# A decoder layer in seven-product block matmuls: the scheme carried from the down projection to gate and up

## The chip, the core and the metric

One core of a Trainium2 chip runs the whole kernel. The metric is device time in microseconds (us) of one execution. TensorE is called PE here, its weight loads PEld, VectorE is DVE, ScalarE is ACT, GpSimd is POOL, and SP issues most DMAs.

## The reference

256 tokens of width 2048 pass one layer: a normalised input projection, a convolution group and an attention group, an output projection, and a SwiGLU feed-forward part of width 5632. Only the last part is touched by the change.

```
x = x + rmsnorm(mix, post_mix_norm)
hf = rmsnorm(x, pre_ffn_norm)                                  # 256 x 2048
ff = (silu(hf @ w_gate) * (hf @ w_up)) @ w_down                # 5632 wide inside
x = x + rmsnorm(ff, post_ffn_norm)
```

## The kernel before

**Precision.** Every weight and every activation is split into two float16 parts, a high part (ACT, a scaled copy) and a low part (DVE, scaled source minus high part). One product of a 128x128 activation block with a 128x512 weight block is then three matmuls: high x high, high x low, low x high (`mm3`, and `mm` in the down part). Weight tiles of 1 MB are loaded by SP into `st` (pool `stage`, 4 buffers) and split into `whi` and `wlo` (pool `wsp`, 8 buffers each, 2048 columns). A `whi`/`wlo` buffer comes free when PE has done the last matmul that reads it, an `st` buffer when DVE has read it last.

**Gate and up.** The loop over `j` takes 22 groups of 512 columns, 256 of gate beside 256 of up. Each group needs 16 blocks of the inner dimension (`k`), for two token blocks (`tb`), so 96 matmuls per group, into two of the four PSUM tiles of `ps_acc`. The first two groups run ahead on token block 0 (`LEAD`), while token block 1 of `hf` is still being normalised, split and transposed by DMA. `swiglu(j, ps)` reads the two PSUM tiles, multiplies, splits, and has the result transposed by DMA into `aT`. For ten groups (`FAST`: 0, 2, ... 18) it also forms the sums of activation blocks that the down part needs.

**Down.** Two passes `u` over 1024 output columns each take 22 pairs of inner blocks. A pair of inner blocks, two token blocks and two halves of the columns make a 2x2 by 2x2 block product: eight block products done plainly (`plain`), so 24 matmuls. For the ten pairs in `FAST` Winograd's scheme does it in seven (21 matmuls): some products go into the result tiles `E`, four others (`X, Y, Z, Q`) into the tiles of `ps_tmp`, and four additions on DVE at the end (`fix`) distribute them. It needs sums of weight blocks: `load_pair` splits three blocks as they come (1536 columns), adds blocks in place in `st` (three DVE additions, L730 to L732), and splits the four results (2048 columns). Pairs alternate, a fast one and then a plain one; the last three are plain.

**Order.** A scheduler orders each engine's instructions at build time; each engine then works through its own list in order, and waits on semaphores for the others. A DVE instruction that waits holds all DVE work behind it.

Of the kernel before, what the change touches and what calls it, by code (L numbers as in the profile page):

```python
# [47 lines left out]
A_S = 8.0  # L48


@with_exitstack
def hymba_layer(ctx: ExitStack, tc: tile.TileContext, x, xT, pos, inv_freq, g_pre, w_in, w_lat,
# [15 lines left out]
    arena = const.tile([P, 70 * KB], F32, name="arena")  # L68
# [185 lines left out]
    rs = rstd_of(ss_t, D, 2)  # L254
    nc.vector.tensor_scalar(r_x, rs, 1.0 / (W_S * X_S), None, op0=ALU.mult)
# [324 lines left out]

    mxc_of = flat(mx_h[:, :CB], mx_l[:, :CB])
    x_off = dram.tile([P, NTB, D], F32, name="x_off")
    r_f = const.tile([P, NTB], F32, name="r_f")
    for tb in range(NTB):
# [13 lines left out]
        for j in range(4):  # L598
# [4 lines left out]
            gx = work.tile([P, 512], F32, tag="ss", name=nm("gxf"), bufs=3)  # L603
# [20 lines left out]
    hw3 = region(50, (2, 3, P), F16)  # L624

# [3 lines left out]
    def fast_of(j):  # L629
# [5 lines left out]
    def swiglu(j, ps):  # L635
        fast = j in FAST
        for tb in range(NTB):
            r = r_f[:, tb : tb + 1]
            sg = work.tile([P, 256], F32, tag="A", name=nm("sg"), bufs=3)
            nc.scalar.activation(sg, ps[tb][:, 0:256], AF.Silu, scale=r)  # L640
# [4 lines left out]
            nc.vector.scalar_tensor_tensor(a, ps[tb][:, 256:512], r, sg, op0=ALU.mult, op1=ALU.mult)  # L645
# [15 lines left out]
    LEAD = 2  # L661
    lead = []
    for j in range(NG):
        wgt = Weights(KD, 512).load(w_gu[j], W_S)
        ps = [acc_tile(), acc_tile()]
        if j < LEAD:
            mm3(ps[0:1], hf_of, wgt, (0,))
            lead.append((wgt, ps))
            if j == LEAD - 1:
                for i, (wgt, ps) in enumerate(lead):  # L670
                    mm3(ps[1:2], hf_of, wgt, (1,))
                    swiglu(i, ps)
        else:
            mm3(ps, hf_of, wgt)
            swiglu(j, ps)
# [6 lines left out]
    ssd = const.tile([P, NTB, 4], F32, name="ssd")  # L682

    def down_out(tb, j, ps, f):
        cs = slice(j * 512, (j + 1) * 512)
        nc.vector.tensor_tensor(f, ps, f, op=ALU.add)
# [4 lines left out]

    r_fin = {}
# [192 lines left out]
```

## Time and profile before

| what | value |
|---|---|
| median of three runs | 1016.5 us (1015.99 to 1017.17) |
| the profiled execution | 1016.03 us, of which its span 1014.2 us |
| PE busy | 975.7 us, 4652 matmuls |
| DVE, ACT busy | 742.5 us, 532.5 us |

The span runs from the first to the last instruction in the trace. Stages by the trace: input projection, convolution and attention up to about 250 us, output projection to about 327 us, gate and up to 784 us, down to about 1001 us, and the last normalisation.

### The profile page before, as it was taken

How to read it: one execution, taken by the hardware profiler on the slowest of the kernel's cores; microseconds unless marked ns; L12 is line 12 of the kernel's file. 1: busy time of each engine (PE TensorE's matmuls, PEld its weight loads, DVE VectorE, ACT ScalarE, POOL GpSimd, SP SyncE). 2: the span in 40 equal slices, each digit the busy share in tenths (PEclk: the TensorE clock that was granted, in tenths of full speed). 3: DMA queues.
4: the chain of work that ended last, by engine and by line, in shares of the span. 5: the costliest groups of instructions: out<-in, count | busy, mean ns of one | idle time of the engine just before them, and what ended most of it. 6: DMA issues, size and time to landing. Idle time of an engine off the chain costs nothing.

```text
span 1014.2 us, 11941 instructions
## 1 busy us (share of the span) xinstructions
PE 975.7 (96%) x4652; PEld 462.3 (46%) x4652; DVE 742.5 (73%) x860; ACT 532.5 (53%) x599; POOL 37.7 (4%) x50
## 2 busy tenths in 40 slices
PE   6999997999999999999999999999999999989996
PEld 2444553774444444444444444444444444434442
DVE  6699999999868886555455555555556788888787
ACT  7796665664746564454444444454443544554551
POOL 0000000034100100000000000000000000000000
PEclk9999998999999999999999999999999999999998
DMA  9874666576546998676766776777755555635453
GB/s 348 330 256 140 223 209 196 166 241 222 201 166 170 321 303 290 218 228 201 240 217 206 222 224 223 226 218 217 234 198 166 176 189 224 235 127 222 166 186 145
DMA packets 77769, 220.37 MB, mean 217 GB/s; under 512 B 49552, under 2 KB 50192, under 8 KB 55184
## 3 DMA queue, kind: packets, MB, share of 16 engines
q1 hardware_dynamic: 76992, 218.68, 64.2%
q10 hardware_dynamic: 720, 0.93, 0.3%
q8 instruction: 36, 0.59, 0.2%
q14 instruction: 21, 0.17, 0.1%
HBM read 204.25 MB, written 4.19 MB: 206 GB/s over the span
## 4 chain that ended last, share of the span: by engine, by line
PE 64%; DVE 18%; issue 5%; ACT 5%; POOL 2%; DMA 1%; DVEq 0%; POOLq 0%; ACTq 0%; SPq 0%
PE acc L146 16%; PE acc L145 16%; PE acc L144 16%; DVE wlo L100 7%; DVE arena L277 3%; PE acc L749 3%; PE acc L750 3%; PE acc L748 3%; ACT whi L99 3%; DVE st L730 1%; PE tmp L749 1%; PE tmp L750 1%; PE tmp L748 1%; POOL sm L198 1%; DVE arena L285 1%
## 5 line engine op out<-in xcount | busy, mean ns | idle before, releaser
L100 DVE SCALAR_TENSOR_TENSOR wlo<-st,whi 128x2048 f16<-128x2048 f32 (+4 forms) x211 | 451.7, 2157 | 203.3 <-ACT whi L99 203.3
L99 ACT ACTIVATE whi<-st 128x2048 f16<-128x2048 f32 (+4 forms) x211 | 376.2, 1800 | 320.7 <-PE acc L146 176.5
L144 PE MATMUL acc<-whi,arena 128*128 128x512 f16 (+1 forms) x1084 | 410.1, 378 | 5.5 <-ACT whi L99 5.5
L145 PE MATMUL acc<-wlo,arena 128*128 128x512 f16 (+1 forms) x1084 | 410.4, 379 | 3.9 <-DVE wlo L100 3.8
L146 PE MATMUL acc<-whi,arena 128*128 128x512 f16 (+1 forms) x1084 | 409.8, 378 | 0.0
L144 PEld LDWEIGHTS <-arena 128*128 128x128 f16 x1084 | 106.7, 98 | 130.2 <-ACT arena L104 4.9
L146 PEld LDWEIGHTS <-arena 128*128 128x128 f16 x1084 | 106.7, 98 | 129.6 <-issue 6.9
L145 PEld LDWEIGHTS <-arena 128*128 128x128 f16 x1084 | 106.5, 98 | 125.2 <-issue 2.5
L748 PE MATMUL acc<-whi,arena 128*128 128x512 f16 x232 | 87.9, 379 | 0.0
L749 PE MATMUL acc<-wlo,arena 128*128 128x512 f16 x232 | 87.9, 379 | 0.0
L750 PE MATMUL acc<-whi,arena 128*128 128x512 f16 x232 | 87.9, 379 | 0.0
L277 DVE SCALAR_TENSOR_TENSOR arena<-arena 128x256 f32<-128x256 f32 x184 | 78.0, 480 | 0.0
L640 ACT ACTIVATE sg<-acc,r_f 128x256 f32<-128x256 f32 x44 | 20.7, 473 | 58.8 <-PE acc L146 58.8
L749 PEld LDWEIGHTS <-arena 128*128 128x128 f16 x272 | 26.6, 98 | 32.3 <-issue 0.3
L748 PEld LDWEIGHTS <-arena 128*128 128x128 f16 x272 | 26.6, 98 | 32.1
L750 PEld LDWEIGHTS <-arena 128*128 128x128 f16 x272 | 26.6, 98 | 32.1
L283 ACT ACTIVATE x_sb<-arena 128x256 f32<-128x256 f32 x56 | 25.2, 506 | 11.7 <-DVE arena L285 11.7
L705 POOL TENSOR_TENSOR sm<-sm,neg_half 128x1 f32<-128x1 f32 x2 | 1.1, 541 | 657.0 <-DVE sm L703 657.0
L730 DVE TENSOR_TENSOR st<-st 128x1024 f32<-128x1024 f32 x20 | 24.5, 1224 | 0.6
L153 PE MATMUL tmp<-arena,whi 128*128 128x256 f16 x80 | 21.8, 273 | 0.0
L154 PE MATMUL tmp<-arena,whi 128*128 128x256 f16 x80 | 21.8, 273 | 0.0
L155 PE MATMUL tmp<-arena,wlo 128*128 128x256 f16 x80 | 21.8, 273 | 0.0
(186 smaller groups left out, 610.1 us busy)
## 6 DMA issues: line engine op xcount, KB each, us to landing
st<-in_w_gu SPq DMA_DIRECT2D x88, 1024.0 KB, 5.0
st<-in_w_dn SPq DMA_DIRECT2D x44, 1024.0 KB, 4.9
st<-in_w_out SPq DMA_DIRECT2D x16, 1024.0 KB, 5.1
st<-in_w_in SPq DMA_DIRECT2D x14, 1024.0 KB, 9.3
st<-in_w_lat SPq DMA_DIRECT2D x12, 896.0 KB, 5.0
x_sb<-in_x SPq DMA_DIRECT2D x4, 1024.0 KB, 8.7
st<-in_w_uqn SPq DMA_DIRECT2D x4, 768.0 KB, 4.9
st<-in_w_uv SPq DMA_DIRECT2D x2, 1024.0 KB, 6.0
```

Source lines behind the costliest of these rows:

```text
L99: nc.scalar.activation(hi, src, AF.Copy, scale=scale)
L100: nc.vector.scalar_tensor_tensor(lo, src, scale, hi, op0=ALU.mult, op1=ALU.subtract)
L144: nc.tensor.matmul(p_ap, xh, wh, start=(start and k == 0), stop=False)
L145: nc.tensor.matmul(p_ap, xh, wl, start=False, stop=False)
L146: nc.tensor.matmul(p_ap, xl, wh, start=False, stop=(stop and k == wgt.kt - 1))
L153: nc.tensor.matmul(ps, wh[:, c0 : c0 + P], xh, start=(k == 0), stop=False)
L277: nc.vector.scalar_tensor_tensor(cacc[:, cb, :], upad[:, cb, k : k + S], cw[:, cb, k : k + 1], cacc[:, cb, :], op0=ALU.mult, op1=ALU.add)
L283: nc.scalar.activation(t[:, i, :], upad[:, cb, k : k + S], AF.Copy, scale=cw[:, cb, k : k + 1])
L730: nc.vector.tensor_tensor(st[:, 0:4:3, :], st[:, 0:2, :], st[:, 3:4, :].to_broadcast([P, 2, 512]), op=ALU.add)
L748: nc.tensor.matmul(ps, ah, bh, start=key not in begun, stop=False)
L749: nc.tensor.matmul(ps, ah, bl, start=False, stop=False)
L750: nc.tensor.matmul(ps, al, bh, start=False, stop=last)
```

## The change

Gate and up are regrouped from 22 groups of 512 columns into 11 units of 1024 columns (`NU`; a unit is two groups `j`). A unit takes 8 pairs of inner blocks, and its weights come as 1 MB per pair, four blocks of 512 columns. In five units (`GU_UNITS`: 1, 3, 5, 7, 9) five of the eight pairs (0 to 4) go through the seven-product scheme; the other pairs and units stay plain. Three things come with it. The sums of `hf` blocks are formed and transposed once, in `hf_sums`, called between token block 0 and token block 1 of unit 0. The `Feed` class makes the weight parts in a set order (blocks of this pair and of the next one before the sums of this pair), and chains these instructions on ACT and on DVE so that the scheduler can't reorder them among themselves. `Unit` takes its result tiles in turn from `ps_acc` and `ps_tmp`, and its four extra tiles from the other pool. In a fast unit the pairs come in the order 5, 0, 1, 6, 2, 3, 4, 7, so a plain one first. In the down part a plain pair now comes ahead of each fast one, and two plain pairs in place of three are kept for the end.

```diff
+NU = NG // 2
+GU_UNITS = (1, 3, 5, 7, 9)
+GU_FAST = 5
...
+    row_s = const.tile([P, NTB], F32, name="row_s")
+    nc.vector.tensor_scalar(row_s, rs, 1.0, None, op0=ALU.min)
...
+    def sized(tb, j):
+        cs = slice(j * 512, (j + 1) * 512)
+        gx = work.tile([P, 512], F32, tag="ss", name=nm("gxf"), bufs=3)
+        nc.vector.scalar_tensor_tensor(gx, x_sb[:, tb, cs], row_s[:, tb : tb + 1], g_pf[:, cs], op0=ALU.mult, op1=ALU.mult)
+        return gx
...
-            nc.vector.tensor_tensor(gx, xs, g_pf[:, cs], op=ALU.mult)
-            split(hl[:, 0, :], hl[:, 1, :], gx, X_S)
+            split(hl[:, 0, :], hl[:, 1, :], sized(tb, j), X_S)
...
+    def hf_sums(c):
+        g0, g1 = [sized(tb, c).rearrange("p (i k t) -> p i k t", i=2, k=2) for tb in range(NTB)]
+        sm = region(44, (4, 2, P))
+        for d, p, m in ((0, g1[:, :, 0], g1[:, :, 1]), (1, g0[:, :, 0], g1[:, :, 0]),
+                        (2, g0[:, :, 0], sm[:, 0]), (3, g0[:, :, 1], sm[:, 2])):
+            nc.vector.tensor_tensor(sm[:, d], p, m, op=ALU.subtract)
+        hl = region(48, (2, 8 * P), F16)
+        split(hl[:, 0, :], hl[:, 1, :], sm.rearrange("p s i t -> p (s i t)"), X_S)
+        nc.sync.dma_start_transpose(hS[:, c], hl.rearrange("p a n -> p (a n)"))
...
+        def blocks(self, k):
+            src, scale, fast = self.pairs[k]
+            st = stage.tile([P, 2048], F32, tag="stage", name=nm("st")).rearrange("p (b n) -> p b n", b=4)
+            nc.sync.dma_start(st, src)
+            self.parts[k] = self.split(st, 1536 if fast else 2048, scale)
+            if fast:
+                b12 = st[:, 3:4, :].to_broadcast([P, 2, 512])
+                for d, p, m in ((st[:, 0:4:3, :], st[:, 0:2, :], b12), (st[:, 1, :], st[:, 0, :], st[:, 1, :]),
+                                (st[:, 2, :], st[:, 1, :], st[:, 2, :])):
+                    self.chain("DVE", nc.vector.tensor_tensor(d, p, m, op=ALU.add))
+                self.st[k] = st
+        def get(self, k, ahead=1):
+            for n in range(k, min(k + ahead + 1, len(self.pairs))):
+                if n not in self.parts:
+                    self.blocks(n)
+            parts = self.parts[k]
+            if k in self.st:
+                parts = parts + self.split(self.st.pop(k), 2048, self.pairs[k][1])
+            return parts
...
+            mine, other = (acc_tile, tmp_tile) if Unit.count % 2 == 0 else (tmp_tile, acc_tile)
...
+        def fast(self, blocks, w, last):
+            if self.sums is None:
+                self.sums = [self.other() for _ in range(4)]
+            X, Y, Z, Q = self.sums
+            A22, A11, A12, S1, S3, S2, S4 = blocks
+            self.mm(self.E[0][0], (0, 0), A12, w[2])
+            self.mm(self.E[0][1], (0, 1), S4, w[1])
+            self.mm(X, "X", A11, w[0], last)
+            self.mm(Y, "Y", S2, w[4], last)
+            self.mm(Z, "Z", S3, w[6], last)
+            self.mm(Q, "Q", S1, w[3], last)
+            self.mm(self.E[1][0], (1, 0), A22, w[5])
...
-    LEAD = 2
-        wgt = Weights(KD, 512).load(w_gu[j], W_S)
-            mm3(ps, hf_of, wgt)
-            swiglu(j, ps)
+    gu_order = [GU_FAST, 0, 1, GU_FAST + 1] + list(range(2, GU_FAST)) + list(range(GU_FAST + 2, KP))
+        if u == 0:
+            ws = [feed.get(i, 0) for i in range(KP)]
+            for tb in range(NTB):
+                for i, w in enumerate(ws):
+                    for c in range(2):
+                        unit.plain(i, w, tb, c, i == KP - 1)
+                if tb == 0:
+                    for c in range((GU_FAST + 1) // 2):
+                        hf_sums(c)
...
-    order = [i for f, s in zip(FAST, slow) for i in (f, s)] + slow[len(FAST) :]
+    order = [i for f, p in zip(FAST, slow) for i in (p, f)] + slow[len(FAST) :]
-    TAIL = 3
+    TAIL = 2
```

How the instructions stand on two engines, at the two places of which the prediction speaks. A row names a line, an operation, the output and inputs (with the tile's number) and the size; in brackets it names what the instruction waits for. The line numbers are those of each kernel.

DVE before, where the first two groups of gate and up end: splits of group 2 (L100), then the gates of the first two groups' results (L645) and the first sum of activation blocks (L655).

```order
L100 SCALAR_TENSOR_TENSOR wlo_3224<-st_3221,whi_3223 128x2048 [waits DMAHW1_49,Activation_49]
L100 SCALAR_TENSOR_TENSOR wlo_3230<-st_3227,whi_3229 128x2048 [waits DMAHW2_49,Activation_49]
L100 SCALAR_TENSOR_TENSOR wlo_3236<-st_3233,whi_3235 128x2048 [waits DMAHW3_49,Activation_49]
L645 SCALAR_TENSOR_TENSOR arena<-acc_2970,r_f,sg_3144 128x256 [waits Activation_49]
L645 SCALAR_TENSOR_TENSOR a_3207<-acc_3043,r_f,sg_3205 128x256 [waits Activation_49]
L655 TENSOR_TENSOR arena<-arena 128x128 [waits DVE_49]
```

DVE after, in the same stretch, at the end of unit 0: unit 1's first splits (L695), the additions in `st` (L709), the sums of `hf` (L669, L109), and the gates of unit 0 (L796). `wlo_3312` holds the weight sums of unit 1's first fast pair.

```order
L695 SCALAR_TENSOR_TENSOR wlo_3305<-st_3302,whi_3304 128x1536 [waits DMAHW3_49,Activation_49]
L709 TENSOR_TENSOR st_3302<-st_3302 128x2x512 [waits DVE_49]
L109 SCALAR_TENSOR_TENSOR arena<-arena 128x1024 [waits DMAHW4_49,Activation_49]
L709 TENSOR_TENSOR st_3302<-st_3302 128x512 [waits DVE_49]
L796 SCALAR_TENSOR_TENSOR arena<-acc_2950,r_f,sg_3227 128x256 [waits DVE_49]
L709 TENSOR_TENSOR st_3302<-st_3302 128x512 [waits DVE_49]
L695 SCALAR_TENSOR_TENSOR wlo_3312<-st_3269,whi_3311 128x2048 [waits PE_49]
L695 SCALAR_TENSOR_TENSOR wlo_3343<-st_3340,whi_3342 128x2048 [waits DMAHW1_49,Activation_49]
L796 SCALAR_TENSOR_TENSOR arena<-acc_2952,r_f,sg_3230 128x256 [waits Activation_49]
L796 SCALAR_TENSOR_TENSOR a_3245<-acc_2951,r_f,sg_3243 128x256 [waits Activation_49]
```

The first fast pair's splits, the sums of `hf` and the gates of unit 0 now stand in one line on DVE, and the gate of `acc_2951` (token block 0, second half) is the last row here; before, the gates of the first groups stood behind plain splits alone.

DVE before, one round of the down loop: a plain pair (`wlo_7017`), the blocks of a fast pair (`wlo_7047`), its three additions, its sums (`wlo_7054`).

```order
L100 SCALAR_TENSOR_TENSOR wlo_7017<-st_7014,whi_7016 128x2048 [waits DMAHW2_49,Activation_49]
L100 SCALAR_TENSOR_TENSOR wlo_7047<-st_7044,whi_7046 128x1536 [waits DMAHW3_49,Activation_49]
L730 TENSOR_TENSOR st_7044<-st_7044 128x2x512 [waits DVE_49]
L731 TENSOR_TENSOR st_7044<-st_7044 128x512 [waits DVE_49]
L732 TENSOR_TENSOR st_7044<-st_7044 128x512 [waits DVE_49]
L100 SCALAR_TENSOR_TENSOR wlo_7054<-st_7044,whi_7053 128x2048 [waits Activation_49]
```

DVE after, one round of the same loop: the blocks of a fast pair (`wlo_7340`), its additions, the next plain pair (`wlo_7373`), then the sums (`wlo_7377`).

```order
L695 SCALAR_TENSOR_TENSOR wlo_7340<-st_7337,whi_7339 128x1536 [waits DMAHW1_49,Activation_49]
L709 TENSOR_TENSOR st_7337<-st_7337 128x2x512 [waits DVE_49]
L709 TENSOR_TENSOR st_7337<-st_7337 128x512 [waits DVE_49] x2
L695 SCALAR_TENSOR_TENSOR wlo_7373<-st_7370,whi_7372 128x2048 [waits DMAHW2_49,Activation_49]
L695 SCALAR_TENSOR_TENSOR wlo_7377<-st_7337,whi_7376 128x2048 [waits Activation_49]
```

The plain pair's split moved from ahead of the blocks to between the additions and the sums. PE's own list is 150 rows shorter, 75 matmuls and their 75 weight loads.

## Rows read from the trace of the kernel before

**Rows 1.** The page's span and busy line (busy us, share, count).

```profile
span 1014.2 us, 11941 instructions
...
PE 975.7 (96%) x4652; PEld 462.3 (46%) x4652; DVE 742.5 (73%) x860; ACT 532.5 (53%) x599; POOL 37.7 (4%) x50
```

**Rows 2.** Windows: busy us and count of PE, PEld, DVE, ACT, POOL; clock, DMA share, GB/s.

```profile
400.00:500.00 100.00, 100.00 (x465) 45.36 (x464) 54.58 (x48) 44.78 (x40) 0.00 (x0) 1.00 0.70 219
790.00:840.00 50.00, 50.00 (x233) 22.67 (x232) 41.28 (x30) 21.22 (x13) 0.00 (x0) 1.00 0.59 212
890.00:940.00 50.00, 46.77 (x217) 21.02 (x216) 40.66 (x34) 25.08 (x22) 0.00 (x0) 1.00 0.44 169
```

**Rows 3.** Waits of PE from 280 to 1000 us (total, times, longest).

```profile
PE acc L748 <- DVE m L686: 3.2, 1, 3.2
PE acc L145 <- DVE wlo L100: 1.5, 1, 1.5
PE tmp L749 <- DVE wlo L100: 1.1, 1, 1.1
```

**Rows 4.** Groups of instructions by line and shape (count; busy us, mean ns; idle before).

```profile
L100 DVE SCALAR_TENSOR_TENSOR wlo<-st,whi 128x2048 f16<-128x2048 f32 x165 | 375.8, 2290 | 197.3 <-ACT whi L99 197.3
...
L100 DVE SCALAR_TENSOR_TENSOR wlo<-st,whi 128x1536 f16<-128x1536 f32 x24 | 42.0, 1752 | 4.7 <-ACT whi L99 4.7
...
L730 DVE TENSOR_TENSOR st<-st 128x1024 f32<-128x1024 f32 x20 | 24.5, 1224 | 0.6
...
L732 DVE TENSOR_TENSOR st<-st 128x512 f32<-128x512 f32 x20 | 13.8, 692 | 0.7
...
L645 DVE SCALAR_TENSOR_TENSOR a<-acc,r_f,sg 128x256 f32<-128x256 f32 x24 | 11.5, 482 | 10.2 <-ACT sg L640 10.2
...
L100 DVE SCALAR_TENSOR_TENSOR wlo<-st,whi 128x1024 f16<-128x1024 f32 x8 | 9.7, 1218 | 0.9 <-ACT whi L99 0.9
...
L601 DVE SCALAR_TENSOR_TENSOR x_sb<-arena,sm,x_sb 128x512 f32<-128x512 f32 x8 | 5.7, 747 | 1.1 <-POOL sm L198 1.1
...
L389 DVE TENSOR_TENSOR qt<-zq,sincos 128x256 f32<-128x256 f32 x2 | 0.8, 416 | 0.0
```

**Rows 5.** DVE's timeline where gate and up begin (start us, us).

```profile
327.95 2.28 DVE L100 SCALAR_TENSOR_TENSOR wlo<-st,whi 128x2048 f16<-128x2048 f32 x1
330.15 0.74 DVE L591 SCALAR_TENSOR_TENSOR arena<-acc,r_c,arena 128x512 f32<-128x512 f32 x1
...
344.32 2.28 DVE L100 SCALAR_TENSOR_TENSOR wlo<-st,whi 128x2048 f16<-128x2048 f32 x1
...
349.81 0.15 DVE L612 TENSOR_SCALAR r_f<-sm 128x1 f32<-128x1 f32 x1 [0.66 <-POOL sm L198]
```

**Rows 6.** PE's timeline there.

```profile
346.65 0.38 PE L145 MATMUL acc<-wlo,arena 128*128 128x512 f16 x1 [1.47 <-DVE wlo L100]
```

**Rows 7.** DMA issues: KB each, median us to landing.

```profile
st<-in_w_gu SPq DMA_DIRECT2D x88, 1024.0 KB, 5.0
...
arena<-arena SPq DMA_TRANSPOSE x14, 5.7
```

**Rows 8.** The chain that ended last, one round of the down loop (start us, us).

```profile
942.19 3.96 DVE wlo L100 x2
...
948.97 1.92 ACT whi L99
...
953.12 3.96 DVE wlo L100 x2
```

**Rows 9.** Windows (columns as in rows 2) around two waits of PE.

```profile
160.00:164.00 4.00, 1.00 (x3) 0.51 (x4) 2.87 (x15) 3.66 (x9) 1.16 (x2) 0.55 0.53 189
164.00:168.00 4.00, 4.00 (x13) 1.61 (x12) 4.00 (x11) 1.04 (x2) 0.00 (x0) 0.59 0.34 65
894.00:896.00 2.00, 0.34 (x2) 0.19 (x2) 2.00 (x3) 1.39 (x2) 0.00 (x0) 1.00 0.04 8
```

More of the change, by code (lines that the diff above doesn't have):

```diff
@@ L67, in hymba_layer @@
     KB = 256
[L68 removed]
+    arena = const.tile([P, 82 * KB], F32, name="arena")
     def region(kb, shape, dtype=F32):
@@ new lines, in hymba_layer, with __init__, chain, split @@
+    class Feed:
+        def __init__(self, pairs):
+            self.pairs = pairs
+            self.parts = {}
+            self.st = {}
+            self.last = {}
+        def chain(self, engine, ins):
+            if engine in self.last:
+                tc.add_manual_dep(ins.ins, self.last[engine].ins.name, NO_SYNC, reason="feed order")
+            self.last[engine] = ins
+        def split(self, st, n, scale):
+            hi = wsp.tile([P, 2048], F16, tag="whi", name=nm("whi"))
+            lo = wsp.tile([P, 2048], F16, tag="wlo", name=nm("wlo"))
+            src = st.rearrange("p b n -> p (b n)")[:, :n]
+            self.chain("ACT", nc.scalar.activation(hi[:, :n], src, AF.Copy, scale=scale))
+            self.chain("DVE", nc.vector.scalar_tensor_tensor(lo[:, :n], src, scale, hi[:, :n],
+                                                             op0=ALU.mult, op1=ALU.subtract))
+            return [(hi[:, c : c + 512], lo[:, c : c + 512]) for c in range(0, n, 512)]
+        def blocks(self, k):
[17 more added lines that the diff above has]
+            return parts
@@ L636, in swiglu @@
+    def swiglu(j, unit, c):
         fast = j in FAST
@@ L715, in final @@
             (nc.sync if j % 2 == 0 else nc.scalar).dma_start(out[tb * P : (tb + 1) * P, cs], xs)
-    def parts_of(st, n):
-        hi = wsp.tile([P, 2048], F16, tag="whi", name=nm("whi"))
-        lo = wsp.tile([P, 2048], F16, tag="wlo", name=nm("wlo"))
-        split(hi[:, :n], lo[:, :n], st.rearrange("p b n -> p (b n)")[:, :n], WD_S)
-        return [(hi[:, c : c + 512], lo[:, c : c + 512]) for c in range(0, n, 512)]
-    def load_pair(u, i):
-        st = stage.tile([P, 2048], F32, tag="stage", name=nm("st")).rearrange("p (b n) -> p b n", b=4)
-        nc.sync.dma_start(st, w_dn[u, i])
-        if i not in FAST:
-            return parts_of(st, 2048)
-        parts = parts_of(st, 1536)
-        nc.vector.tensor_tensor(st[:, 0:4:3, :], st[:, 0:2, :], st[:, 3:4, :].to_broadcast([P, 2, 512]), op=ALU.add)
-        nc.vector.tensor_tensor(st[:, 1, :], st[:, 0, :], st[:, 1, :], op=ALU.add)
-        nc.vector.tensor_tensor(st[:, 2, :], st[:, 1, :], st[:, 2, :], op=ALU.add)
-        return parts + parts_of(st, 2048)
@@ L788, in hymba_layer @@
+        unit = Unit(a_of)
+        k0 = NU * KP + u * NG
+        for n, i in enumerate(order[:-TAIL]):
+            w = feed.get(k0 + n)
+            if i in FAST:
+                unit.fast(a_fast(i), w, i == FAST[-1])
+            else:
+                unit.plain_all(i, w)
+        tail = [(i, feed.get(k0 + NG - TAIL + n)) for n, i in enumerate(order[-TAIL:])]
         if u == 1:
@@ L791, in hymba_layer @@
                 nc.sync.dma_start(x_back[tb], x_off[:, tb, :])
-        i, w = tail[0]
         for tb in range(NTB):
             for c in range(2):
-                plain(i, w, tb, c)
-        for tb in range(NTB):
-            for c in range(2):
-                for i, w in tail[1:]:
-                    plain(i, w, tb, c, i == order[-1])
-                down_out(tb, 2 * u + c, E[tb][c], fix[tb][c])
+                for i, w in tail:
+                    unit.plain(i, w, tb, c, i == order[-1])
+                down_out(tb, 2 * u + c, unit.block(tb, c))
                 if u == 1 and c == 0:
```

138 lines of the change are left out of this document (74 added, 64 removed).

## The prediction

> **What bounds the kernel now.** First the page's busy line: PE is busy 96% of the span, DVE 73%, ACT 53% [rows 1]. A share is a mean over stages, so next the windows. From 400 to 500 us, in gate and up, PE is busy without a gap and starts 465 matmuls in 100 us, one per 0.215 us, at granted clock 1.00, its upper level of 2.4 GHz; in the first half of the down part it is the same 233 in 50 us [rows 2]. In these stretches DVE is busy 55% and 83%, DMA 70% and 59%. So PE sets the time here, and a matmul less is 0.215 us less, as long as nothing else comes late. PE's waits between 280 and 1000 us are the list of what is late today: 1.5 us for a weight split where gate and up begin, 3.2 us at the border of the two down passes, 1.1 us near the end of the second [rows 3].
>
> **The change part by part.**
>
> *Matmuls.* 5 units x 5 pairs x one block product x 3 matmuls = 75 fewer. 75 x 0.215 = 16.1 us less, all on the engine that bounds.
>
> *Where DVE has to follow.* A plain pair costs DVE one split of 2048 columns, 2.29 us; a fast one a split of 1536 (1.75), additions of 1.22 and twice 0.69, and a split of 2048 (2.29), 6.65 us in all [rows 4]. Back to back, instructions start about 0.08 us closer than their durations (327.95 to 330.15 is 2.20 for one of 2.28 [rows 5]). A fast unit thus asks 5 x 6.4 + 3 x 2.2 = 39 us of DVE for weights, plus some 11 us for gates, sums and the eight additions of the scheme, 50 us against PE's 177 x 0.215 = 38.1. A plain unit asks 8 x 2.2 + 5 = 23 us against 192 x 0.215 = 41.3. Two units together: 73 of 79.4 us. DVE can do it if it works ahead during the plain unit. I followed one such border in the two engines' lists. With eight `whi`/`wlo` buffers, DVE has everything ready up to the blocks of pair 2 when PE begins a fast unit (call that 0). The gates of the unit before, with their subtractions and splits, hold DVE to about 3.6; then blocks of 3 (4.3, to 8), sums of 2 (2.2, to 10), blocks of 4 (14.5), sums of 3 (17), pair 7 (19). The sums of 4 need the buffer that pair 6 gives back at 19, and then ACT's 1.9 and DVE's 2.2: 24. PE wants the three sums at 21, 26 and 30. So units 3, 5, 7 and 9 lose nothing by it. The border behind a fast unit holds too: the four extra tiles are read about 5 us after the last product into them, and PE spends that time on pair 7.
>
> *Unit 1, where nothing could be done ahead.* Unit 0 holds all eight buffers until its second pass, and DVE has the sums of `hf` to make in that very stretch. DVE's list from the last split of unit 0 to the gate of token block 0, second half, whose PSUM tile product Y of the first fast pair wants: nine operations of 512 columns on `hf` (0.67 or 0.61, 5.9 us), twelve subtractions of 256 (at most 0.35 by the 0.42 of L389: 4.2), three splits of 1024 (1.15: 3.4), three of 2048 (6.6), two of 1536 (3.3), additions 2 x 1.24 and 4 x 0.7 (5.3), three gates (0.40: 1.2), small ones with a wait for POOL (0.9): 30.8 us [rows 4, 5]. In the trace that last split starts at 344.3 and PE goes on at 346.65 [rows 5, 6]; I take 347.0, since seven multiplications ahead of it turn into the three-operand form (0.75 in place of 0.69). So 377.8 without any stall. PE, from 347.0: 11 matmuls of the first pass, 96 of the second, 24 of pair 5 and 9 of the first fast pair, 140 x 0.215, wants the tile at 377.1. From there DVE needs 22.5 us more to the sums of pair 3 (the rest of unit 0's gates and splits 3.0, the blocks of pairs 2, 3 and 4 with their additions 3 x 4.3, the sums of pairs 1, 2 and 3 3 x 2.2): 400.3. PE's second pass ends at 370.0, and 24 + 21 + 21 + 24 + 21 + 9 = 120 matmuls later, at 395.8, it wants them. The loss in unit 1 is then some 4.5 us without any stall. More comes from ACT: the second and third split of `hf` sums reuse one buffer, which must have been transposed by DMA first. No row shows a transpose of 2048 columns; the ones of half the width and less land 5.7 us after issue [rows 7]. At that figure ACT waits some 1 to 2 us for each, and DVE behind it in part; at twice that, some 6 us more. Also, the load of a pair lands 5.0 us after its buffer comes free [rows 7], and a gate's split stands behind such a load on ACT: 1 us. I take 6.5 us, since the transposes seen lie near the low end; the bounds are 2.5 (a little work done in gaps that I don't see) and 12.
>
> *Down.* In the trace a round of a fast and a plain pair in the second pass takes DVE 10.9 us (942.19 to 953.12), with 2 us in it in which DVE only waits for ACT to make the high parts of the sums [rows 8]; PE needs 45 x 0.215 = 9.7. The stock of splits is eaten up, hence the 1.1 us. In the new order the plain pair's split of 2.2 us stands in that place: 2.2 + 1.7 + 1.24 + 1.4 + 2.2 = 8.8 us, below 9.7. The 3.2 us at the border come from result tiles that the second pass reuses while DVE has yet to read them; with `Unit` the second pass writes into the tiles of X, Y, Z, Q instead, which are read 5 us earlier. Both waits go, 4.3 us; if something else turns up in their place, 0. I take 4.3, since neither has another instruction close behind it in the lists.
>
> *Front.* Three operations of two columns on DVE near 35 us, hidden while DVE is half busy there; the three-operand form above, 0.4 us.
>
> *Sum.* 1016.0 (profiled execution, 1.8 us beyond its span) - 16.1 + 6.5 - 4.3 + 0.4 = 1002.5. The median of the runs lies 0.5 above the profiled one: **1003.0 us**.
>
> **A rule on the clock.** From 160 to 164 us PE was busy 1 us of 4, then with 13 matmuls in 4 us, and the granted clock fell to 0.55 and 0.59, near the lower level of 1.2 GHz; right at the 3.2 us wait of the down part it stayed 1.00 [rows 3, 9]. My stalls in unit 1 are pieces of 1 to 4 us, so the sum has none of this. The Trainium skill ("TensorE: Matmul & The Clock Gate", What's actually happening) says that the throttled state is the default and activity releases it, which speaks against adding idle spells to a stage that had none. By that rule the sum would be the third rival's; by the row at 3.2 us it stays.
>
> **The rivals.**
>
> 1. *Unit 1 doesn't stall*: the sums land early, DVE catches up. 1016.5 - 16.1 - 4.3 = 996. For it: the DVE count misses PE by 0.7 us only at the first point. Against: it misses by 4.5 us at the later one, without any stall counted.
> 2. *The waits in the down part stay*, in another place: 1003 + 4.3 = 1007. For it: DVE at 8.8 of 9.7 us has little to spare. Against: today's loop at 10.9 lost only 1.1 us.
> 3. *The clock falls in unit 1*: of the 8 us at 0.57 [rows 9], 3.4 us were lost; 1003 + 3.4 = 1006.5. For it: several waits close together. Against: the row at 3.2 us.
> 4. *Slower: DVE sets the pace in every fast unit.* Mechanism: a fast pair takes two of eight buffers and keeps its `st` until the sums are made, so DVE can't work ahead enough. Then each fast unit takes DVE's 50 us, not PE's 38: 12 us lost in each of units 3, 5, 7, 9, and 1003 + 48 = 1051. It turns slower than before from 3.4 us a unit on. For it: 73 of 79 us on two units leaves 8%. Against: the border followed above has 6 to 11 us in hand. The Trainium skill ("Perfetto Trace Analysis", Optimization Strategy) reads the same gap recurring on an engine that should be full as too few buffers for the next tile; today's windows show no such gap, and this rival is what it would look like.
>
> That the change doesn't do what it says can be left out: PE's list is 150 rows shorter, 75 of them matmuls.
>
> **How the numbers follow.** Forecast 63%, rival 1 10%, rival 2 9%, rival 3 10%, rival 4 8%. The forecast's own bounds are 1016.5 - 16.1 + 2.5 - 4.3 + 0.4 = 999 and, with 12 us in unit 1, 1008.5. The range 998 to 1009 takes in rivals 2 and 3 and leaves out 1 and 4. What can be told from no change is 0.2%, 2 us. Below 1014.5 lie the first four cases: 0.89. Within 2 us only a mild form of rival 4: 0.03. Above: 0.08.
>
> **What would show it.** PE: 4577 matmuls, still one per 0.215 us outside unit 1. DVE busy some 890 us (742 + 25 x 4.36 for the fast pairs + 27 for the scheme's additions + 13 for the sums of `hf`). PE's waits: 4 to 9 us between 377 and 405, for gates (L796) and splits (L695); none at the later unit borders; none over 1 us in the down part until its end. If waits recur in units 3 to 9, rival 4 holds; if the clock is below 1.00 near 380, rival 3; if PE's gap near 377 is missing, rival 1. The forecast would be wrong altogether if a shorter list of matmuls came with longer gaps between them.

## The result, and the profile after

The changed kernel takes 1001.4 us (median of four runs, 999.0 to 1001.6), the kernel before 1016.8 in the same comparison: a ratio of 0.984, with a 95% interval of 0.983 to 0.986. It is 15 us faster. The forecast was 1003.0.

The profiled execution took 1001.55 us, its span is 14.5 us shorter than before. Span and busy line of the page after, to set beside [rows 1]:

```profile
span 999.7 us, 11980 instructions
...
PE 959.6 (96%) x4577; PEld 454.4 (45%) x4577; DVE 876.3 (88%) x1024; ACT 578.1 (58%) x632; POOL 33.6 (3%) x50
```

PE makes 75 matmuls less and is as full as before; DVE has 134 us more work, now 88% of the span. The same windows as in [rows 2], of the kernel after:

```profile
400.00:500.00 100.00, 98.02 (x453) 44.29 (x453) 90.30 (x84) 58.68 (x48) 0.00 (x0) 1.00 0.74 263
500.00:600.00 100.00, 100.00 (x465) 45.30 (x463) 93.96 (x94) 56.27 (x51) 0.00 (x0) 1.00 0.71 236
...
790.00:840.00 50.00, 50.00 (x233) 22.63 (x232) 45.28 (x34) 27.93 (x16) 0.00 (x0) 1.00 0.58 223
890.00:940.00 50.00, 50.00 (x234) 22.66 (x232) 47.27 (x35) 28.22 (x16) 0.00 (x0) 1.00 0.57 216
```

465 matmuls in 100 us is the old pace, with DVE at 94% beside it; only the first window is short, by 12 matmuls. The waits of PE from 280 to 1000 us (total, times, longest), which answer to [rows 3]:

```profile
PE acc L740 <- DVE wlo L695: 4.7, 3, 2.2
PE acc L739 <- DVE q L773: 1.4, 1, 1.4
PE acc L739 <- DVE a L796: 0.7, 1, 0.7
PE tmp L557 <- DVE arena L552: 0.6, 1, 0.6
PE acc L739 <- DVE m L770: 0.4, 1, 0.4
```

Both waits of the down part are gone, and no new one stands there. The 0.6 us of L557 stand at 285 us, ahead of gate and up, and the kernel before has the same wait there (L545, 0.6 us), which [rows 3] doesn't list. Where the others are, from PE's timeline after:

```profile
347.23 0.38 PE L740 MATMUL acc<-wlo,arena 128*128 128x512 f16 x1 [2.22 <-DVE wlo L695]
...
379.60 0.39 PE L739 MATMUL acc<-whi,arena 128*128 128x512 f16 x1 [0.69 <-DVE a L796]
...
393.56 0.38 PE L740 MATMUL acc<-wlo,arena 128*128 128x512 f16 x1 [0.62 <-DVE wlo L695]
...
400.14 0.38 PE L740 MATMUL acc<-wlo,arena 128*128 128x512 f16 x1 [1.89 <-DVE wlo L695]
...
493.73 0.38 PE L739 MATMUL acc<-whi,arena 128*128 128x512 f16 x1 [0.40 <-DVE m L770]
...
497.92 0.38 PE L739 MATMUL acc<-whi,arena 128*128 128x512 f16 x1 [1.44 <-DVE q L773]
```

The first is the old wait of [rows 6], 0.7 us longer. The next three are unit 1: the gate of token block 1, second half, then the sums of pairs 2 and 3. Counted from start to start of PE's matmuls, less the usual 0.215 us, PE lost 0.86, 0.79 and 2.05 us there, 3.7 in all. (The list has 0.17 less for each: it counts from the end of the matmul ahead, which it puts 0.38 us behind that one's start.) The last two are new, where fast unit 3 ends and plain unit 4 begins: 2.2 us, counted in the same way. From start to start PE's second down pass takes 112.3 us before and 107.5 after, 4.8 less, where the two old waits are 4.3 in the list. The ledger: - 16.1 (75 x 0.215) + 3.7 + 0.7 + 2.2 - 4.8 = -14.3 of the -14.5 us by which the span moved. The 0.2 left over stands ahead of gate and up, which begin at 326.5 in place of 326.7 us.

What DVE does in unit 1, from its timeline after:

```profile
344.89 2.29 DVE L695 SCALAR_TENSOR_TENSOR wlo<-st,whi 128x2048 f16<-128x2048 f32 x1
...
354.39 1.22 DVE L109 SCALAR_TENSOR_TENSOR arena<-arena 128x1024 f16<-128x1024 f32 x1
...
361.52 1.22 DVE L109 SCALAR_TENSOR_TENSOR arena<-arena 128x1024 f16<-128x1024 f32 x1
...
369.40 1.23 DVE L109 SCALAR_TENSOR_TENSOR arena<-arena 128x1024 f16<-128x1024 f32 x1
...
379.07 0.47 DVE L796 SCALAR_TENSOR_TENSOR a<-acc,r_f,sg 128x256 f32<-128x256 f32 x1
```

The three rows of L109 are the splits of the `hf` sums. From 344.89 to past 397 us DVE stops once, for 0.44 us (for POOL, as in [rows 5]); no transpose and no load holds it. And at the end of unit 3, DVE's timeline after:

```profile
486.73 2.29 DVE L695 SCALAR_TENSOR_TENSOR wlo<-st,whi 128x2048 f16<-128x2048 f32 x1 [1.20 <-ACT whi L694]
490.78 2.29 DVE L695 SCALAR_TENSOR_TENSOR wlo<-st,whi 128x2048 f16<-128x2048 f32 x1 [1.76 <-ACT whi L694]
492.99 0.68 DVE L770 TENSOR_TENSOR m<-xs,acc 128x512 f32<-128x512 f32 x1
...
494.38 2.28 DVE L695 SCALAR_TENSOR_TENSOR wlo<-st,whi 128x2048 f16<-128x2048 f32 x1
...
497.18 0.68 DVE L773 TENSOR_TENSOR q<-acc,n 128x512 f32<-128x512 f32 x1
```

The combinations of X, Y, Z, Q (L770 to L773), which free the PSUM tiles that unit 4 writes, stand in DVE's list behind splits of unit 4. These wait for ACT, and ACT for the load:

```profile
488.84 1.91 ACT L694 ACTIVATE whi<-st 128x2048 f16<-128x2048 f32 x1 [2.15 <-DMA st<-in_w_gu]
```

How far ahead DVE is can be worked out from the two timelines: the time from the end of DVE's split of a pair's sums to PE's first matmul with them (low parts are wanted 0.2 us later still). For the changed kernel, in us:

```
             pair 0   pair 1   pair 2   pair 3   pair 4
unit 1          3.0      0.6     -0.9     -2.2      0.0
unit 3         10.2     10.3      5.2      3.2      3.3
unit 5         18.4     17.6      9.9      7.9      8.0
unit 7         22.4     17.6      9.9      7.9      8.0
unit 9         21.2     17.6      9.9      7.9      8.0
down, from its second fast pair on: 14 to 18 in the first pass, 12 to 15 in the second
```

### The profile page after: what moved, and what is told of

Read it like the earlier page. It is cut to its first block, busy times and chain, and to the rows that moved or that the text cites. A ratio compares the mean times of both kernels' runs of the same rounds, so it can differ in the third digit from the quotient of the medians.

```text
span 999.7 us, 11980 instructions
## 1 busy us (share of the span) xinstructions
PE 959.6 (96%) x4577; PEld 454.4 (45%) x4577; DVE 876.3 (88%) x1024; ACT 578.1 (58%) x632; POOL 33.6 (3%) x50
## 4 chain that ended last, share of the span: by engine, by line
PE 60%; DVE 23%; issue 5%; ACT 4%; DMA 3%; POOL 1%; SPq 0%; DVEq 0%; POOLq 0%; ACTq 0%
PE acc L740 10%; PE acc L741 10%; PE acc L739 10%; PE tmp L741 6%; PE tmp L740 6%; PE tmp L739 6%; DVE wlo L695 6%; DVE arena L289 3%; DVE wlo L109 3%; DVE st L709 2%; PE acc L155 2%; PE acc L153 2%; PE acc L154 2%; DMA st<-in_w_gu 2%; POOL sm L207 1%
## 5 line engine op out<-in xcount | busy, mean ns | idle before, releaser
L694 ACT ACTIVATE whi<-st 128x2048 f16<-128x2048 f32 (+1 forms) x177 | 317.1, 1798 | 228.7 <-PE acc L741 77.6
L695 DVE SCALAR_TENSOR_TENSOR wlo<-st,whi 128x2048 f16<-128x2048 f32 (+1 forms) x177 | 375.2, 2150 | 52.9 <-ACT whi L694 52.5
L740 PE MATMUL acc<-wlo,arena 128*128 128x512 f16 x620 | 235.0, 379 | 4.7 <-DVE wlo L695 4.7
L739 PE MATMUL acc<-whi,arena 128*128 128x512 f16 x620 | 235.0, 379 | 2.5 <-DVE q L773 1.4
L741 PE MATMUL acc<-whi,arena 128*128 128x512 f16 x620 | 235.0, 379 | 0.0
L153 PE MATMUL acc<-whi,arena 128*128 128x512 f16 (+1 forms) x380 | 143.5, 378 | 5.5 <-ACT whi L108 5.5
L154 PE MATMUL acc<-wlo,arena 128*128 128x512 f16 (+1 forms) x380 | 143.4, 377 | 2.2 <-DVE wlo L109 2.0
L155 PE MATMUL acc<-whi,arena 128*128 128x512 f16 (+1 forms) x380 | 143.3, 378 | 0.0
L739 PE MATMUL tmp<-whi,arena 128*128 128x512 f16 x331 | 125.4, 379 | 0.0
L740 PE MATMUL tmp<-wlo,arena 128*128 128x512 f16 x331 | 125.4, 379 | 0.0
L741 PE MATMUL tmp<-whi,arena 128*128 128x512 f16 x331 | 125.4, 379 | 0.0
L109 DVE SCALAR_TENSOR_TENSOR wlo<-st,whi 128x2048 f16<-128x2048 f32 (+4 forms) x59 | 118.2, 2009 | 6.5 <-ACT whi L108 6.5
L709 DVE TENSOR_TENSOR st<-st 128x1024 f32<-128x1024 f32 x135 | 117.2, 868 | 4.1
L108 ACT ACTIVATE whi<-st 128x2048 f16<-128x2048 f32 (+4 forms) x59 | 98.5, 1677 | 34.4 <-PE acc L155 10.3
```

What stands on the lines that cost most here:

```text
L108: nc.scalar.activation(hi, src, AF.Copy, scale=scale)
L109: nc.vector.scalar_tensor_tensor(lo, src, scale, hi, op0=ALU.mult, op1=ALU.subtract)
L153: nc.tensor.matmul(p_ap, xh, wh, start=(start and k == 0), stop=False)
L154: nc.tensor.matmul(p_ap, xh, wl, start=False, stop=False)
L155: nc.tensor.matmul(p_ap, xl, wh, start=False, stop=(stop and k == wgt.kt - 1))
L694: self.chain("ACT", nc.scalar.activation(hi[:, :n], src, AF.Copy, scale=scale))
```

## The experiments

Ratios are to the kernel before on the same chip, with 95% intervals; it took 1016.1 us beside the first four kernels, 1015.5 beside the next four and 1015.6 beside the last four.

**Undoing parts of gate and up.** No fast unit at all:

```diff
-GU_UNITS = (1, 3, 5, 7, 9)
+GU_UNITS = ()
-                if tb == 0:
+                if tb == 0 and GU_UNITS:
```

> All eleven units of gate and up take eight products, and the sums of hf are not made; all else is as in the changed kernel (order of splits, down part with its two passes in each other's tiles). PE makes 4652 matmuls as before. My theory: what is left is the down part, 4.3 us of waits gone, and about 0.4 us more at the front: 1016.8 - 4.3 + 0.4 = 1012.9 us, no PE wait over 1 us in the down part. Rival: the gain in the down part comes only with the fast units (another rhythm of splits when the down part begins), so that here the waits are back: 1016.8, with a wait of 3 us at the border of the two passes.

Measured: 1011.2 us, ratio 0.9958 (0.9944 to 0.9972), so 4.3 us less than before by the ratio (2.8 to 5.7) and 4.9 by the medians. PE's waits in 280 to 1000 us are the one near 347 us, in unit 0, and the one at 285 us:

```profile
PE acc L740 <- DVE wlo L695: 2.2, 1, 2.2
PE tmp L557 <- DVE arena L552: 0.6, 1, 0.6
```

The gain of the down part comes with or without fast units in gate and up: PE's second pass takes 107.5 us here too. Then one fast unit alone, 1 or 5:

```diff
-GU_UNITS = (1, 3, 5, 7, 9)
+GU_UNITS = (1,)     # e2;  (5,) in e3
```

> Only unit 1 is fast; the sums of hf are made as in the changed kernel. PE makes 4637 matmuls, 15 fewer than the plain version: 3.2 us. My theory: unit 1 costs what the trace of the changed kernel shows as its waits there, 3.7 us, so this stands at the plain version's time + 0.5 us, with the same PE waits near 380, 394 and 400 us. Rival: unit 1's waits are only put off by what other units do, or are hidden by a plain unit behind it: the plain version - 3.2 us.

> Only unit 5 is fast, and the sums of hf, made beside unit 0, have all the time until then. 15 matmuls fewer than the plain version. My theory: DVE has worked ahead by then and nothing waits: the plain version - 3.2 us; the wait of 2 us that the changed kernel has where unit 3 ends is of unit 3's place in the load rhythm, not of each fast unit. Rival: each fast unit pays a border where the four combinations of X, Y, Z, Q stand behind splits on DVE: the plain version - 1.2 us, with PE waiting some 2 us for them where unit 6 begins. A second rival: the sums of hf themselves cost time beside unit 0, whoever uses them: then less than that is gained, with the loss before 380 us.

Measured: unit 1 alone 1012.0 us, 0.9960 (0.9945 to 0.9975); unit 5 alone 1009.2 us, 0.9932 (0.9914 to 0.9951). Against the plain version's 0.9958, unit 1 gains nothing: its 3.2 us of matmuls are paid back in the waits, which are those of the changed kernel (4.7 us in 3 for splits, 0.7 for the gate). Unit 5 gains 2.6 us by the ratios, with no PE wait behind the one near 347 us, its own borders included. So the border is not a price of each fast unit. The times alone, between 1.2 and 3.2 us, would not have told that; the list of waits does.

The other half of the places:

```diff
-GU_UNITS = (1, 3, 5, 7, 9)
+GU_UNITS = (2, 4, 6, 8, 10)
```

> The five fast units are 2, 4, 6, 8 and 10 in place of 1, 3, 5, 7 and 9: the same 4577 matmuls. Unit 1 is plain, so DVE makes the sums of hf and works ahead before the first fast unit. My theory: the 3.7 us of unit 1 go: the changed kernel - 3.7 us, some 997.7 us. Rival: unit 10 has the down part's first fast pairs right behind it, so DVE has no plain unit to catch up in, and as much is lost there as unit 1 lost: within 1 us of the changed kernel, with PE's waits now near 800 us.

Measured: 996.1 us, 0.9806 (0.9791 to 0.9821), with the same two waits as the plain version and no others. The profiled span is 993.8 us, 5.9 us under the changed kernel's: the 3.7 us of unit 1 went as expected, and the 2.2 us behind unit 3 with them. Unit 10 costs nothing: DVE's lead at the second fast pair of the down part is 5 us where the changed kernel has 18, and it doesn't run dry.

**What holds DVE back in unit 1.** Two things meet there: DVE makes the sums of `hf`, and unit 0 holds the split buffers. The first can be left out:

```diff
-        s = [(hS[:, i // 2, 2 * b + i % 2, :], hS[:, i // 2, 8 + 2 * b + i % 2, :]) for b in range(4)]
+        s = [hf_of(2 * i + b % 2, b // 2) for b in range(4)]
...
-                if tb == 0:
-                    for c in range((GU_FAST + 1) // 2):
-                        hf_sums(c)
```

> The changed kernel, but the seven blocks of hf in a fast pair are all read from the four that are there; the sums of hf (nine operations of 512 columns, twelve subtractions, three splits and three transposes) are left out, so the product is another one. The matmuls, the splits of weights and the units are the same. My theory: unit 1 loses its 3.7 us because DVE makes the sums of hf, 13.5 us, in the stretch in which it would have to work ahead: without them DVE comes 13.5 us earlier and the 3.7 us go: the changed kernel - 3.7 us. Rival: DVE can't work ahead anyway, since unit 0 holds all eight split buffers until its second pass reads them and each new load needs 5 us: the waits for splits at 394 and 400 us stay, at least 2.5 of the 3.7 us.

Measured: 996.2 us, 0.9811 (0.9794 to 0.9827), and no wait at all in unit 1: the buffers are not what binds. (ACT's splits of the sums and their transposes are left out with them, but the rows above show DVE held by neither, so it is DVE's work that counts.) The wait at the end of unit 3 is gone too. DVE's smallest lead in unit 3 is 7.8 us there, not 3.2: the backlog of unit 1 had not been made good by unit 3, and without it the wait at 494 to 498 us doesn't come.

**The border behind unit 3, by another way.** The changed kernel again as a control, and beside it a version in which the copy of X and the four combinations have a set place in the chains of ACT and DVE:

```diff
+        def finish(self, feed):
+            feed.chain("ACT", nc.scalar.copy(xs_, X))
+            feed.chain("DVE", nc.vector.tensor_tensor(m, xs_, Y, op=ALU.subtract))
...
+                    if n == KP - 1 and unit.sums is not None:
+                        unit.finish(feed)
...
+        unit.finish(feed)                # in the down part, behind the splits of the last two pairs
```

> The changed kernel again, so that the three beside it are compared on one chip: 0.984 of before, as in its first measurement; PE waits of 4.7, 1.4, 0.7 and 0.4 us (splits, q, gate, m) if the pattern is of the program, other ones at the end of unit 3 if that wait hangs on when loads land.

> The copy of X and the four combinations of X, Y, Z, Q get a set place in ACT's and DVE's order, behind the first split of the next unit's first pair, in place of one that the scheduler picks, which at the end of unit 3 put them behind splits that wait for loads. My theory: the 2.0 us at the border of units 3 and 4 go, the rest stays: the changed kernel - 2.0 us. Rival: the combinations then stand ahead of splits that PE wants as soon, or ahead of PE's last product and hold DVE: no gain, or a wait for splits of up to 2 us where units 2, 4, 6 begin.

Measured: control 1000.4 us, 0.9853 (0.9836 to 0.9869), with the same waits, 1.0 us in place of 1.8 behind unit 3; the chained version 998.6 us, 0.9832 (0.9817 to 0.9847), with none there. So this wait is not of the program alone. In the changed kernel, the control and the two down experiments below (e6, e7; their gate and up are untouched) ACT waits 2.15, 1.50, 0.54 and 2.38 us for the load in front of that border, and PE behind it 1.8, 1.0, 0.2 and 1.9 us. The chained version takes away just that border: PE needs 85.7 us for units 0 and 1 together in it and in the control. (Its list has 1.8 us of waits in unit 1 in place of 3.2, because there the granted clock fell near 347 us and PE came later; see the last section.) A gain of 2.1 us with intervals of 1.6 on each side would not show it by itself. DVE's timeline in the chained version tells its price:

```profile
484.17 0.69 DVE L772 TENSOR_TENSOR m<-xs,acc 128x512 f32<-128x512 f32 x1 [4.09 <-ACT xs L770]
```

The combinations come 9 us earlier, but DVE stands still for 4.1 us until PE is done with X. Its smallest lead in later units is 5 to 7 us instead of 8, and 4 instead of 12 in the second down pass: enough here.

The same chaining on top of the even units:

```diff
-GU_UNITS = (1, 3, 5, 7, 9)
+GU_UNITS = (2, 4, 6, 8, 10)   # together with finish()
```

> Fast units 2, 4, 6, 8, 10 together with the set place for the copy and the four combinations. My theory: nothing is left for the set place to take away, since the version with even units has no PE wait behind 350 us: 0.9806 of before, within 1 us of that version. Rival: the 2 us come on top, since borders lose something that the waits don't show: some 994 us.

Measured: 998.0 us, 0.9821 (0.9806 to 0.9836); the even version had 0.9806. No gain, as expected, since nothing waited there. I had it within 1 us of the even version, and it is 1.5 us slower by the ratios. The intervals overlap, but the trace shows where it loses. DVE stands still for X behind unit 10 as well, which has no plain unit behind it, and PE then waits in the first pairs of the down part, where DVE's lead in the even version is 12 and 5 us. DVE's row, then PE's:

```profile
763.12 0.69 DVE L772 TENSOR_TENSOR m<-xs,tmp 128x512 f32<-128x512 f32 x1 [4.42 <-ACT xs L770]
```

```profile
777.44 0.59 PE L739 MATMUL acc<-whi,x_sb 128*128 128x512 f16 x2 [0.17 <-ACT whi L694]
...
779.90 0.38 PE L740 MATMUL acc<-wlo,x_sb 128*128 128x512 f16 x1 [0.36 <-DVE wlo L695]
...
789.02 0.38 PE L740 MATMUL acc<-wlo,x_sb 128*128 128x512 f16 x1 [0.32 <-DVE wlo L695]
```

The first down pass takes PE 108.8 us here against 107.5 in every other version: 1.3 us.

**What made the down part faster.** The prediction gave the 3.2 us at the border of its passes to the tiles, the 1.1 us at the end to the order. Each is undone alone.

```diff
-            w = feed.get(k0 + n)
+            w = feed.get(k0 + n, 0)      # e6: no next pair ahead of the sums
...
     for u in range(2):
+        Unit.count = NU                  # e7: both passes in the same tiles
         unit = Unit(a_of)
```

> In the down part the split of the next, plain pair no longer stands ahead of a fast pair's sums: in DVE's list the sums' split comes right behind the additions, and DVE has to wait for ACT there, as before the change. Gate and up are untouched. My theory: a round is 10.9 us on DVE again against PE's 9.7, the stock of splits is eaten up, and PE waits for sums in the second half of each pass: 1 to 4 us more than the changed kernel. Rival: the order is worth nothing since the stock lasts: within 0.5 us of the changed kernel, without a PE wait in the down part.

> The second pass of the down part writes its four plain results into the same four PSUM tiles as the first pass, not into those of X, Y, Z and Q. My theory: PE waits again 3.2 us at the border of the passes, for the combinations that read these tiles: the changed kernel + 3.2 us. Rival: the wait went by the new order of splits, since DVE now reaches the combinations earlier: no change.

Measured: without the order 1007.8 us, 0.9931 (0.9911 to 0.9950); without the tiles 1001.3 us, 0.9854 (0.9839 to 0.9868), against the control's 1000.4 and 0.9853. So the tiles are worth nothing here and the order is worth 7 us, more than the two old waits together. I missed both sizes: I had 3.2 for the one and at most 4 for the other.

What stands behind that is when DVE has freed the result tile that comes last at this border, and when PE wants it, in us (worked out from the two timelines):

```
                      freed by DVE   wanted by PE   in hand
before                   895.6          892.3        -3.3
changed kernel           884.3          890.3         6.0
same tiles (e7)          884.7          886.1         1.4
old order (e6)           889.5          888.8        -0.7
```

The other tiles give PE 4 to 5 us more, but with the new order, and a plain pair first that takes up the tiles one by one over 3.9 us, DVE is in time without them. In e6, where DVE is late and the tiles are the new ones, the stop at the border is 0.6 us in place of 3.2, and the second pass then pays. DVE's and PE's timelines of e6 in that pass:

```profile
935.84 6.16 DVE L695 SCALAR_TENSOR_TENSOR wlo<-st,whi 128x2048 f16<-128x2048 f32 x3 [2.06 <-ACT whi L694]
...
946.77 6.16 DVE L695 SCALAR_TENSOR_TENSOR wlo<-st,whi 128x2048 f16<-128x2048 f32 x3 [2.06 <-ACT whi L694]
```

```profile
938.18 0.38 PE L740 MATMUL tmp<-wlo,x_sb 128*128 128x512 f16 x1 [0.98 <-DVE wlo L695]
...
949.11 0.38 PE L740 MATMUL tmp<-wlo,x_sb 128*128 128x512 f16 x1 [1.06 <-DVE wlo L695]
...
960.04 0.38 PE L740 MATMUL tmp<-wlo,x_sb 128*128 128x512 f16 x1 [1.06 <-DVE wlo L695]
```

A round takes 10.93 us on both engines: DVE's pace of [rows 8], with its 2.06 us of waiting for ACT, against the 9.7 that PE needs. DVE's lead, worked out as above, falls by 1.2 us a round through both passes: 13.9 at the third fast pair of the first pass, then 12.7, 11.5, 10.3 and so on to 5.4; 3.5 at the second fast pair of the second pass, and -1.3 at the sixth, where PE's waits begin. In the changed kernel it is 12 to 15 at all these places. From start to start PE's second pass takes 115.0 us in e6 and 107.5 in the control: five rounds of 10.93 in place of 9.7, 1.0 us at the border and 0.5 at the end of the pass, 7.5 in all. By the medians e6 loses 7.4. The kernel before had the same losing round, began to wait for splits only at 986 us and lost 4.8 us in this pass; that its 3.2 us stop gave DVE lead for the second pass would explain it, but was not tried by itself.

**The rival that makes it slower.** The same number of fast units, without plain ones between them:

```diff
-GU_UNITS = (1, 3, 5, 7, 9)
+GU_UNITS = (3, 4, 5, 6, 7)
```

> The five fast units are 3, 4, 5, 6 and 7, with no plain unit between them: the same 4577 matmuls. My theory: a fast unit asks 50 us of DVE against PE's 38.1, as the prediction counted; alternating with plain units that is hidden, in a row it isn't: 12 us lost in each of units 4 to 7, less the 6 to 11 us that DVE is ahead when unit 3 begins, is some 37 to 42 us, so about 996 + 40 = 1036 us, with PE waiting for splits in every pair of units 4 to 7. Rival: what limits DVE is waiting for ACT and loads at the borders, not its work, so in a row it costs less than half of that: under 1016 us.

Measured: 1025.8 us, 1.0096 (1.0080 to 1.0111): slower than before, 30 us above the even version with the same matmuls. PE's waits from 480 to 680 us:

```profile
PE acc L740 <- DVE wlo L695: 11.7, 6, 4.6
PE tmp L740 <- DVE wlo L695: 10.2, 6, 4.6
```

and one of them once a unit, from PE's timeline:

```profile
521.02 0.38 PE L740 MATMUL tmp<-wlo,arena 128*128 128x512 f16 x1 [1.89 <-DVE wlo L695]
...
569.20 0.38 PE L740 MATMUL acc<-wlo,arena 128*128 128x512 f16 x1 [1.89 <-DVE wlo L695]
...
617.49 0.38 PE L740 MATMUL tmp<-wlo,arena 128*128 128x512 f16 x1 [1.89 <-DVE wlo L695]
...
665.79 0.38 PE L740 MATMUL acc<-wlo,arena 128*128 128x512 f16 x1 [1.89 <-DVE wlo L695]
```

From one of these waits to the next DVE takes 48.2 us, busy 44.6 of every 45 us, against PE's 38.1 alone for a fast unit. I had counted 50. The gap that recurs at the same place of each unit is what, by the Trainium skill ("Perfetto Trace Analysis", Optimization Strategy), can mean that buffers for the next tile are lacking. Here DVE is busy nearly all the time, so the trace decides for DVE's work; a version with more buffers was not run. The total is 30 and not 40 us, since only three such periods stand there, not four: the lead that DVE has in unit 3 covers most of unit 4, where PE loses 2.5 us up to 521.0 us. In the three periods PE makes 193, 177 and 177 matmuls (the scheduler takes its products in another order here), which at 0.215 us leaves 6.7, 10.2 and 10.2 us lost: 29.6 in all. After that, in plain unit 8, PE waits no more.

**One more fast pair.** With DVE's lead at 8 us in the even version there is room:

```diff
-GU_UNITS = (1, 3, 5, 7, 9)
-GU_FAST = 5
+GU_UNITS = (2, 4, 6, 8, 10)
+GU_FAST = 6
-    gu_order = [GU_FAST, 0, 1, GU_FAST + 1] + list(range(2, GU_FAST)) + list(range(GU_FAST + 2, KP))
+    gu_order = [GU_FAST] + list(range(GU_FAST)) + list(range(GU_FAST + 1, KP))
```

> Units 2, 4, 6, 8 and 10 with six fast pairs of eight in place of five, one plain pair ahead of them and one behind: 4562 matmuls, 15 fewer again. DVE asks 4.2 us more per fast unit, 77 of PE's 78.7 us for two units. My theory: that still fits, and it gains 3.2 us on the version with even units: some 993 us. Rival: with only one plain pair behind a fast unit and DVE at 98% the stock doesn't come back, and splits are late in each fast unit from the second on: no gain, or up to 2 us lost in each of four units, 996 to 1004 us.

Measured: 992.7 us, 0.9773 (0.9758 to 0.9787), the fastest of all. The page, and the only wait of PE from 340 to 1030 us:

```profile
PE 957.0 (96%) x4562; PEld 453.8 (46%) x4562; DVE 895.1 (90%) x1044; ACT 584.7 (59%) x637; POOL 38.0 (4%) x50
```

```profile
PE acc L740 <- DVE wlo L695: 2.2, 1, 2.2
```

DVE's smallest lead is 5.0 us in each of the five fast units alike, so the stock does come back; it falls to 2.4 us where the down part begins and recovers from there.

## Why the prediction was right, and where it was not

*Matmuls, - 16.1.* Right: 4577 matmuls, and 465 in 100 us where nothing waits.

*Unit 1, + 6.5.* Right in kind, too large: 3.7. The list of DVE's work was good: the gate that Y waits for was forecast for 377.8 us and done at 377.4, the one that PE then stopped for, the last of unit 0, at 379.5; the sums of pair 3 were forecast for 400.3 and came at 400.1. What failed is the step that added 2 us for ACT waiting on the transposes and on a load, with DVE held behind it. The three new transposes land 4.3 us after issue, not 5.7, and the trace of before had others of half the width, those of `hl`, that landed in 4.1, which the prediction passed over:

```profile
L672 SPq DMA_TRANSPOSE arena<-arena x3: 1830/1925/2200, 355.6 to 370.6; - x3
...
DMA to landing us min/median/max: 4.3/4.3/4.3
```

(issue times in ns, first and last start). ACT did stand still for 2.6 us ahead of the second split of sums, until the first transpose had landed near 359.9 us (a split of DVE ended in the same 0.1 us). But the splits that reuse the buffer stand 7 to 8 us apart in DVE's list, with other work between them, so DVE never waited. The other 0.8 us is the difference between 4.5 and 3.7: DVE was ready 0.2 us earlier, PE without its first two stops came 0.4 later than counted, and it wants the low part 0.2 later than the high one. The sign that the prediction gave, waits of 4 to 9 us, was missed with it: they are 3.2 in the list. The cause, the sums of `hf` on DVE, is shown by e9.

*Later borders, 0.* Wrong by 2.2 us at one of four. In units 5, 7 and 9 the border went as followed: forecast leads of 11, 9 and 6 us for the sums of pairs 2, 3 and 4, measured 9.9, 7.9 and 8.0. But I started it with "DVE has everything ready" and used that for unit 3 as well, where the backlog of unit 1 was still there (5.2, 3.2, 3.3). And I took the four extra tiles to be read some 5 us after the last product into them, without following where the scheduler puts the combinations among the chained splits: the last product into them ends near 486 us, and DVE reads them until 497.9. e9 and e8 each take the wait away, one by the backlog, one by the place.

*Down, - 4.3.* Right in sum (4.8 from start to start), not in its reason. Both waits went, but for the 3.2 us the tiles are not needed (e7: no difference); the new order of splits is enough for both, and undone it costs 7 us (e6), with 0.6 us of wait left at the border. The count of 10.9 against 9.7 us a round was the right one to follow: over 20 rounds it takes 24 us of DVE's lead, of which 4.8 came out as loss in the kernel before and 7.5 in e6.

*Front, + 0.4.* 0.7 measured, PE's wait near 347 us being 2.2 in place of 1.5 us.

The errors, - 2.8, + 2.2, + 0.3 and - 0.5, cancel to - 0.8: that the total came within 2 us is in part luck. The rest of the 1.6 us between 1003.0 and 1001.4 is the size of what executions of one kernel differ by.

*Two sums beside the forecast.* The chances of the forecast and of rivals 1 to 3 add up to 0.92, not 0.89. And DVE was forecast busy for some 890 us and was for 876: the count added durations, while instructions back to back start some 0.08 us before the profiled end of the one ahead [rows 5]; for the 164 instructions more that is an estimated 13 us.

*The rivals.* The first did not come, since unit 1 did stall; it is what the even units give (996.1 us, where it had 996). The second is out, no wait is left in the down part. The third is out for unit 1, where the clock was 1.00 throughout; in six other executions it fell just ahead of unit 1, and where that unit is fast it cost nothing (last section). The fourth is real as a mechanism, and e10 shows its price, 10 us per unit against the 12 of the prediction; alternating with plain units it doesn't come up.

## What to carry to other kernels

When work is moved from the engine that bounds to one that follows it, count the follower's work over a whole period of the pattern (here 73 of 79 us, which held) and then ask at which place it starts without a stock: that place, not the average, is where time is lost, and moving the pattern by one unit was worth 5 us. A loop in which the follower needs 1.2 us more than the bound engine shows few waits in a profile while its stock lasts; follow its lead round by round, because what it costs depends on the stock with which it begins: the same round lost 4.8 us in the kernel before and 7.5 in e6. Where a scheduler places small operations that free buffers among chained large ones, follow their place too.

## What the runs showed of the hardware

The clock after a wait of PE. After the 2.2 us wait before 347 us the granted clock stays 1.00 in seven profiled executions of the changed kernels and falls in six. The same windows of PE in the changed kernel, where it stays, and in e12, where it falls (busy us, count, clock, DMA share, GB/s):

```profile
344.00:346.00 2.00, 1.01 (x5) 1.00 1.05 162
346.00:348.00 2.00, 0.77 (x4) 1.00 1.20 358
348.00:350.00 2.00, 2.00 (x11) 1.00 0.87 308
350.00:352.00 2.00, 2.00 (x11) 1.00 1.01 191
```

```profile
344.00:346.00 2.00, 1.24 (x6) 1.00 0.92 155
346.00:348.00 2.00, 0.59 (x3) 0.97 1.11 316
348.00:350.00 2.00, 2.00 (x7) 0.50 0.90 341
350.00:352.00 2.00, 2.00 (x8) 0.68 1.01 193
```

From 348 to 352 us that is 15 matmuls in place of 22, 1.5 us. So the row at 3.2 us that kept 1.00 [rows 9] was no proof that such a wait is harmless: with the same wait, the clock went either way from one kernel's execution to another's. The Trainium skill ("TensorE: Matmul & The Clock Gate", What's actually happening) says that throttled is the default and activity releases it; these rows agree in kind. Whether the longer wait here, 2.2 in place of 1.5 us, makes the fall more frequent than before is open. What it costs depends on what follows. Unit 0 takes PE 43.8 us where the clock stays and 45.5 where it falls. But where unit 1 is fast and DVE makes the sums of `hf`, units 0 and 1 together take 85.7 us in all six profiled executions, three with the fall (e6, e7, e8) and three without: DVE decides there, and PE's stops in unit 1 are shorter by what the clock took. Where unit 1 is plain the 1.7 us stay: 85.2 us without the fall (e4) and 86.9 with it (e11, e12). In e10 it fell twice, near the end of waits of 4.6 us that ended at 590.6 and 638.9 us; the first, in the same columns:

```profile
592.00:594.00 2.00, 2.00 (x6) 0.50 0.00 0
```

It cost nothing there: the waits shown above at 521.02, 569.20, 617.49 and 665.79 us, for the same split of each unit, follow each other after 48.18 us with the clock at 1.00 and after 48.29 and 48.30 us with a fall in between, for DVE sets the pace. In the kernels of this study a wait of some microseconds on PE thus cost more than its own length where PE set the pace behind it, and not where DVE did.
